# Token tiles between the modulation's pieces, a diagonal product for the norm, and modulation sums as columns, in the opening of a diffusion trunk layer

## The chip, the cores and the metric

The kernel runs on one core of a Trainium2 chip (trn2). Its engines are TensorE (PE; its weight loads are listed apart as PEld), VectorE (DVE), ScalarE (ACT), GpSimd (POOL) and SyncE (SP), which here issues transfers. The metric is the device time of one execution in microseconds (us), of which the median of several runs is taken.

## The reference

One layer of a trunk: the modulation (six vectors of 1024 from `c`, and those of the context from `c_ctx`), a normed and modulated input for 256 context tokens and 1024 latent tokens, one projection, two token mixers, an output projection, and a gated MLP with a depthwise convolution. All is f32.

```python
mod = jax.nn.silu(c) @ ada_w[l] + ada_b[l]
sh1, sc1, g1, sh2, sc2, g2 = [m[:, None, :] for m in jnp.split(mod, 6, axis=-1)]
csh1, csc1, cg1, csh2, csc2, cg2 = jnp.split(jax.nn.silu(c_ctx) @ ada_w[l] + ada_b[l], 6, axis=-1)
hc = modulate(rms_norm(ctx, norm1_g[l]), csh1, csc1)          # x * rsqrt(mean(x*x) + eps) * g, then h * (1 + scale) + shift
out_c, ctx_states = mixer_block(hc, lp, (zero_state, zero_state), not last)
hx = modulate(rms_norm(x, norm1_g[l]), sh1, sc1)
out_x, _ = mixer_block(hx, lp, ctx_states, True)              # starts with h @ lp["w_in"]
x = x + g1 * out_x
...
```

The modulation is (1024) times (1024 x 6144), `ada_w`; only its first third, shift and scale of the first norm, is wanted before the projection. `w_in` is 1024 x 3328.

## The kernel before

The layer is written as stages. This case is about the opening, up to the first projections (L354).

The 1280 tokens lie in ten tiles of 128 tokens (`xt`, 128 x 1024): two of context, eight of latents. `norm_x(i)` takes a tile's mean square on ACT (L267), makes `rstd` on DVE with one square root on ACT (L163 to L175), scales the tile by it on DVE (L269), transposes its eight blocks on TensorE into the banks `ph` (L273), and copies them out, half on ACT, half on DVE (L274). So the tokens come to lie along the free axis, in `raws`, for three segments: context (256 tokens, g = 0) and two of 512 latents (g = 1, 2), each in two halves q of four blocks.

`load_ada(ci, q)` loads one quarter of one of the modulation's four column pieces (`araw`, 128 x 2 x 512, 512 KB; 16 of them). For pieces 0, 1 and 2 TensorE multiplies it: the two columns of `ccs` (silu of `c` and `c_ctx`) are stationary, 512 columns of `araw` move, and the sums come out as two rows (L248). After a piece's last quarter the rows are copied (`arows`, L251) and turned into columns by four small products (`pcol`, L254), and the bias is added (L255) into `modc`. Piece 3 is summed on DVE (`aacc`, L236, L238) and made into columns by products with a vector of ones (L243). With all four, `gs` (L316) is norm gain times (1 + scale).

Then `raws` is modulated: ACT writes the high half of the split operand `hx` (L326, rounded to fp32r), DVE does the same in f32 in place (L327), and the difference is the low half (L328), on POOL for segment 1, on DVE for the others. The projection multiplies, per block of 128 columns of `w_in` and per segment, 8 blocks of the depth by three products: high by high, high by low, low by high (`pj`, L354; 24 products a segment). The first column block is 3072.

Loads are issued by SP in program order; the twelve small parameter loads into `pr` (L278 to L290) by POOL, through the name `PQ`. Tiles `xt` and `araw` share 17 buffers. The order of loads and norms is the string `XO`: a digit is a quarter of that modulation piece, `x` the next token tile, loaded and normed. A scheduler with a timing model of its own orders the instructions on each engine from this program.

Of the kernel before, what the change touches and what calls it, by code (L numbers as in the profile page):

```python
# [8 lines left out]
F32 = mybir.dt.float32  # L9
F32R = mybir.dt.float32r  # L10
AF = mybir.ActivationFunctionType
ALU = mybir.AluOpType
# [25 lines left out]
PADC, PADM = 88, 80  # L38
PN1 = (5,)
NA = 17  # L40
XO = "xx0300301131x123222x"
AE = (0, 1, 0, 1, 0, 0, 1, 0)
B1 = ((4, 5, 1), (2, 3), (6, 7), (0,), (1,))
B2 = ((2, 3), (1, 6))
# [43 lines left out]
def hybrid_kernel(  # L88
# [6 lines left out]
    nc = tc.nc  # L95
    V, A, G, PE, SY = nc.vector, nc.scalar, nc.gpsimd, nc.tensor, nc.sync

    PQ = G
    turns = lambda: tc.manual_schedule(engines={mybir.EngineType.PE})
    E1, E2, E3, ES = G, G, V, V  # L100
    F1, F2, F3, F4 = (V, G), G, G, G
# [25 lines left out]
    ident = cst[:, C_ID:C_ID + 128]  # L127
# [6 lines left out]
    modc = cp.tile([128, 4, 8, 2], F32, name="modc")  # L134
    gs1 = cp.tile([128, 8, 2], F32, name="gs1")
    gs2 = cp.tile([128, 8], F32, name="gs2")
    ccs = cp.tile([128, 8, 2], F32, name="ccs")
# [23 lines left out]
    def rstd_of(pool, ss, n, scale, eps):  # L161
        v = pool.tile([128, n], F32, name="rvar", bufs=2)
        V.tensor_scalar(out=v, in0=ss, scalar1=scale, scalar2=eps, op0=ALU.mult, op1=ALU.add)  # L163
        return newton(pool, v, n)
# [32 lines left out]
    def seg_tile(g, q, b, dt):  # L197
        n = segs3[g][1]
        return (hxp if g else hcp).tile([128, 4, n], dt, name="hx", tag=f"h{g}{q}{b}", bufs=1)
# [6 lines left out]
    with ExitStack() as s2:  # L206
        np_ = s2.enter_context(tc.tile_pool(name="np", bufs=1, side="left", reuse_waits="tile"))
        pp = Banks(pada=(0, 1), padv=(7,), ph=(2, 3, 4, 5), pcol=(6,))
# [5 lines left out]
        xts = []  # L214

        def load_x(i):
            xt = np_.tile([128, D], F32, name="xt", tag="araw", bufs=NA)
            SY.dma_start(xt, ctx[0, i * 128:(i + 1) * 128, :] if i < 2 else x[0, (i - 2) * 128:(i - 1) * 128, :])
            xts.append(xt)
# [4 lines left out]
        def load_ada(ci, q):  # L224
            raw = np_.tile([128, D], F32, name="araw", bufs=NA).rearrange("p (k n) -> p k n", k=2)
            SY.dma_start(raw, ada_w[0, :, ci * 512:(ci + 1) * 512].rearrange("(p k) n -> p k n", k=8)[:, 2 * q:2 * q + 2, :])
            if q == 0:
                adas[ci] = pp.tile([128, 512], F32, name="pada", tag="padv" if ci == 3 else "pada", bufs=2)
            ps = adas[ci]
            bias = prm[:, P_AB + 4 * ci:P_AB + 4 * ci + 4].unsqueeze(2).to_broadcast([128, 4, 2])  # L230
            if ci == 3:
                for kk_ in range(2):
                    for t in range(2):
                        k, z = 2 * q + kk_, acc[t]
                        if k == 0:
                            V.tensor_scalar(out=z, in0=raw[:, kk_, :], scalar1=ccs[:, k, t:t + 1], scalar2=None, op0=ALU.mult)  # L236
                        else:
                            V.scalar_tensor_tensor(out=z, in0=raw[:, kk_, :], scalar=ccs[:, k, t:t + 1], in1=z, op0=ALU.mult, op1=ALU.add)  # L238
                if q == 3:
                    for b in range(4):  # L240
                        for t in range(2):
                            o = ps[:, 2 * b + t:2 * b + t + 1]
                            PE.matmul(o, acc[t][:, 128 * b:128 * b + 128], cst[:, C_ONE:C_ONE + 1], start=True, stop=True)  # L243
                    V.tensor_tensor(out=modc[:, 1, 4:8, :], in0=ps[:, 0:8].rearrange("p (b t) -> p b t", t=2), in1=bias, op=ALU.add)
                return
            for kk_ in range(2):
                k = 2 * q + kk_
                PE.matmul(ps[0:2, :], ccs[:, k, :], raw[:, kk_, :], start=(k == 0), stop=(k == 7))  # L248
            if q == 3:
                rows = np_.tile([2, 512], F32, name="arows", bufs=2)  # L250
                V.tensor_copy(rows, ps[0:2, :])  # L251
                pc = pp.tile([128, 512], F32, name="pcol", tag="pcol", bufs=1)
                for b in range(4):
                    PE.matmul(pc[:, 2 * b:2 * b + 2], rows[:, 128 * b:128 * b + 128], ident[0:2, 0:2], start=True, stop=True)  # L254
                V.tensor_tensor(out=modc[:, ci // 2, 4 * (ci % 2):4 * (ci % 2) + 4, :], in0=pc[:, 0:8].rearrange("p (b t) -> p b t", t=2), in1=bias, op=ALU.add)  # L255

        ss = np_.tile([128, NT], F32, name="ss")
        junk = np_.tile([128, D], mybir.dt.bfloat16, name="junk", bufs=1)
# [5 lines left out]
        def norm_x(i):  # L264
            g = 0 if i < 2 else 1 if i < 6 else 2
            a = 128 * i - segs3[g][0]
            A.activation(junk, xts[i], AF.Square, accum_out=ss[:, i:i + 1])  # L267
            rs = rstd_of(np_, ss[:, i:i + 1], 1, 1.0 / D, eps6)
            V.tensor_scalar(out=xts[i], in0=xts[i], scalar1=rs, scalar2=None, op0=ALU.mult)  # L269
            for q in range(2):  # L270
                ph = pp.tile([128, 4, 128], F32, name="ph", tag="ph", bufs=4)
                for j in range(4):
                    PE.transpose(ph[:, j, :], xts[i][:, 128 * (4 * q + j):128 * (4 * q + j) + 128], ident)  # L273
                (A.copy, V.tensor_copy)[q](raws[g, q][:, :, a:a + 128], ph)  # L274

        pr = np_.tile([128, 3, 128], F32, name="pr")
        V.memset(pr, 0.0)
        PQ.dma_start(pr[0:8, 0, :], norm1_g[0].rearrange("(j p) -> j p", p=128))  # L278
        PQ.dma_start(pr[78:94, 0, :], ada_b[0, 0:2048].rearrange("(j p) -> j p", p=128))
        PQ.dma_start(pr[8:16, 0, :], norm2_g[0].rearrange("(j p) -> j p", p=128))  # L280
        PQ.dma_start(pr[16:20, 0, :], rw_k_k[0].rearrange("(j p) -> j p", p=128))
        PQ.dma_start(pr[20:24, 0, :], rw_k_a[0].rearrange("(j p) -> j p", p=128))
        PQ.dma_start(pr[24:28, 0, :], rw_r_k[0].rearrange("(j a) p -> j (a p)", a=2))
        PQ.dma_start(pr[28:40, 0, :], conv_a_w[0].rearrange("w (j p) -> (w j) p", p=128))
# [13 lines left out]
        V.tensor_copy(prm[:, 161:260], pt[:, 256:355])  # L298
        V.tensor_scalar(out=prm[:, P_LB:P_LB + 16], in0=pt[:, 62:78], scalar1=0.5, scalar2=None, op0=ALU.mult)
        V.tensor_scalar(out=kac, in0=prm[:, P_KA:P_KA + 4], scalar1=-1.0, scalar2=2.0, op0=ALU.mult, op1=ALU.add)  # L300
        n_ = 0
        i_ = [0] * 4
        for o in XO:
            if o == "x":
                load_x(n_)
                norm_x(n_)
                n_ += 1
            else:
                ci = int(o)
                load_ada(ci, i_[ci])  # L310
                i_[ci] += 1
        while n_ < NT:
            load_x(n_)
            norm_x(n_)
            n_ += 1
        V.scalar_tensor_tensor(out=gs1, in0=modc[:, 1], scalar=1.0,  # L316
                               in1=prm[:, P_N1:P_N1 + 8].unsqueeze(2).to_broadcast([128, 8, 2]), op0=ALU.add, op1=ALU.mult)
        for g, (t0, n, w) in enumerate(segs3):
            for q in range(2):
                o = [seg_tile(g, q, i, F32R) for i in range(2)]  # L320
                hxt[g, q, 0], hxt[g, q, 1] = o
                for jj in range(4):
                    j = 4 * q + jj
                    g_, b_ = gs1[:, j, w:w + 1], modc[:, 0, j, w:w + 1]
                    src = raws[g, q][:, jj, :]
                    A.activation(o[0][:, jj, :], src, AF.Identity, scale=g_, bias=b_)  # L326
                    V.tensor_scalar(out=src, in0=src, scalar1=g_, scalar2=b_, op0=ALU.mult, op1=ALU.add)  # L327
                    (G if g == 1 else V).tensor_tensor(out=o[1][:, jj, :], in0=src, in1=o[0][:, jj, :].bitcast(F32), op=ALU.subtract)  # L328


    cols = [3072] + [b + 128 * j for b in (2048, 2560, 1536) for j in range(4)] + [3200]
# [29 lines left out]
    pp = Banks(pj=PJ1, pn=PN1, pv=(4,), pl=PL1)  # L361

    def stg():
        return sg_.tile([128, 512], F32, name="stg", bufs=STG)
# [17 lines left out]
    for d in range(2):  # L382
# [3 lines left out]
        for i, src in enumerate((rw_w_up, rw_a_up)):  # L386
            raw = stg()
# [483 lines left out]
    pp = Banks(pa=B3, ry=(2, 3), pu=(1, 6), **B4)  # L871
# [183 lines left out]
    for r in range(16):  # L1055
# [3 lines left out]
        if r == RC:  # L1059
            fill(999)  # L1060
            sa.close()
            op = so.enter_context(tc.tile_pool(name="op", bufs=1, side="left", reuse_waits="tile"))
# [18 lines left out]
    pp = Banks(ry=(2, 3), pu=(1, 6), **B5)  # L1081
# [48 lines left out]
    for f in (1, 0, *range(2, NF)):  # L1130
# [13 lines left out]
        for tap in range(9):  # L1144
            a_, b_ = divmod(tap, 3)
            src = gp[:, a_:a_ + 16, b_:b_ + 64]
# [8 lines left out]
        for hf, c0, n, t0 in PIECES:  # L1155
            V.tensor_tensor(out=act[:, t0:t0 + n], in0=pv[hf][:, c0:c0 + n],  # L1156
                            in1=acc.rearrange("p r c -> p (r c)")[:, t0:t0 + n], op=ALU.mult)
# [29 lines left out]
    for th in range(2):  # L1187
# [8 lines left out]
        for q in range(4):  # L1196
# [3 lines left out]
            t = 4 * th + q  # L1200
# [10 lines left out]
            rs = rstd_of(ep, s_[:, 0:1], 1, 1.0 / D, eps6)  # L1211
# [39 lines left out]
```

## Time and profile before

| | |
|---|---|
| device time, median of 3 runs | 1708.09 us (1707.33 to 1716.09) |
| device time of the profiled execution | 1706.38 us |
| span of the profiled execution | 1704.6 us |
| TensorE busy | 1557.3 us, 91% of the span, 10639 matmuls |
| DVE, ACT, POOL busy | 67%, 36%, 33% |
| chain that ended last, by engine | PE 68%, DVE 17%, DMA 7% |
| mean granted TensorE clock | 0.94 |

The profile is of one execution, its times count from the span's start. The granted clock is a share of full speed: 1.00 is 2.4 GHz, 0.50 is 1.2 GHz. An engine's idle time costs something only if it lies on the chain of work that ends last.

### The profile page before, as it was taken

The page shows a single profiled execution, that of the slowest core. Times are in us where ns is not written, and L with a number is a line of the kernel's source. Part 1 is how long each engine was busy: PE and PEld are TensorE (multiplying, and loading weights), DVE is VectorE, ACT ScalarE, POOL GpSimd, SP SyncE. Part 2 cuts the span into 40 slices and gives each one's busy share as a digit, 9 for nine tenths or more (in the row PEclk, how much of TensorE's full clock was granted, in tenths as well). Part 3 has the DMA queues.
Part 4 walks back from the last instruction along what each step waited for, and adds up shares of the span by engine and source line. Part 5 has one row for each costly group of instructions (what it writes and reads, how often), then busy time and mean ns, then how long its engine had stood idle before and what let it go on. Part 6 is the DMA issues. An engine that isn't in the chain of part 4 may idle for free.

```text
span 1704.6 us, 27504 instructions
## 1 busy us (share of the span) xinstructions
PE 1557.3 (91%) x10639; PEld 1258.8 (74%) x10639; DVE 1148.5 (67%) x1783; ACT 619.2 (36%) x1158; POOL 562.6 (33%) x489
## 2 busy tenths in 40 slices
PE   7699999989899866899778889999999999999997
PEld 2588768867777656787666668888888888788886
DVE  4954525798899987444677577777777777446645
ACT  2654315544445335444345331211111111324323
POOL 2343312332333303412444322222222222545643
PEclk9699799989799976999889999999999999999999
DMA  9385536557576487988652211111111111533521
GB/s 320 105 292 170 182 95 208 164 152 247 159 231 209 135 248 221 331 249 279 188 164 85 92 50 50 50 50 48 43 46 50 50 50 50 178 106 124 173 93 57
DMA packets 233147, 246.94 MB, mean 145 GB/s; under 512 B 18483, under 2 KB 171656, under 8 KB 233016
## 3 DMA queue, kind: packets, MB, share of 16 engines
q1 hardware_dynamic: 232632, 245.02, 46.1%
q8 instruction: 84, 1.38, 0.3%
q14 instruction: 47, 0.39, 0.1%
q0 software_dynamic: 384, 0.15, 0.0%
HBM read 178.79 MB, written 66.33 MB: 144 GB/s over the span
## 4 chain that ended last, share of the span: by engine, by line
PE 68%; DVE 17%; DMA 7%; ACT 3%; issue 3%; POOL 2%; SPq 1%; DVEq 0%; ACTq 0%; POOLq 0%
PE pf L1104 26%; PE pj L354 13%; PE pf L1184 12%; PE pco L906 2%; DVE ti L672 2%; DVE tmp L670 2%; PE po L906 2%; PE px L601 2%; DMA araw<-in_ada_w_dram 2%; DVE acc L1151 2%; PE ry L760 1%; PE pu L772 1%; PE ps L784 1%; DMA vu<-v_dram 1%; PE ry L752 1%
## 5 line engine op out<-in xcount | busy, mean ns | idle before, releaser
L1104 PE MATMUL pf<-h,fhi 128*128 128x512 f32 x1408 | 385.1, 390 | 6.7 <-DVE act L1156 4.1
L1104 PEld LDWEIGHTS pf<-h,fhi 128*128 128x128 f32 x1408 | 265.0, 188 | 63.1 <-DVE act L1156 4.5
L354 PE MATMUL pj<-hx,whi 128*128 128x512 f32 (+1 forms) x976 | 301.6, 388 | 0.9 <-DVE hx L328 0.9
L1151 DVE SCALAR_TENSOR_TENSOR acc<-gp,prm,acc 128x1024 f32<-128x1024 f32 x176 | 272.7, 1551 | 6.0
L106 POOL TENSOR_TENSOR flo<-fraw,fhi 128x1024 fp32r<-128x1024 f32 x50 | 124.2, 2485 | 306.0 <-ACT fhi L105 305.9
L1104 PE MATMUL pf<-h,flo 128*128 128x512 f32 x704 | 223.7, 390 | 0.0
L354 PEld LDWEIGHTS pj<-hx,whi 128*128 128x128 f32 x976 | 184.0, 196 | 37.2 <-issue 4.2
L354 PE MATMUL pj<-hx,wlo 128*128 128x512 f32 (+1 forms) x488 | 189.0, 388 | 0.0
L1184 PE MATMUL pf<-dhi,ahl 128*128 128x512 f32 x640 | 163.0, 389 | 0.2 <-DVE ahl L1176 0.2
L1176 DVE TENSOR_TENSOR ahl<-act,ahl 128x512 fp32r<-128x512 f32 x44 | 86.2, 1969 | 100.2 <-ACT ahl L1175 100.2
L1104 PEld LDWEIGHTS pf<-h,flo 128*128 128x128 f32 x704 | 132.5, 188 | 27.5 <-POOL flo L106 0.2
L105 ACT CAST fhi<-fraw 128x1024 fp32r<-128x1024 f32 x50 | 52.7, 1054 | 266.7 <-issue 158.6
L1184 PEld LDWEIGHTS pf<-dhi,ahl 128*128 128x128 f32 x640 | 120.0, 188 | 25.5 <-DVE ahl L1176 0.6
L106 POOL TENSOR_TENSOR dlo<-fraw,dhi 128x1024 fp32r<-128x1024 f32 x40 | 98.6, 2469 | 92.2 <-ACT dhi L105 88.2
L106 POOL TENSOR_TENSOR wlo<-wraw,whi 128x1024 fp32r<-128x1024 f32 x26 | 63.6, 2447 | 159.9 <-ACT whi L105 159.8
L354 PEld LDWEIGHTS pj<-hx,wlo 128*128 128x128 f32 x488 | 95.7, 196 | 17.2 <-issue 1.7
L1149 DVE TENSOR_SCALAR acc<-gp,prm 128x1024 f32<-128x1024 f32 x22 | 42.5, 1932 | 97.3 <-ACT gp L1141 97.3
L650 POOL TENSOR_TENSOR car<-car,pcs 128x512 f32<-128x512 f32 (+1 forms) x38 | 39.3, 1046 | 152.4 <-DMA car<-ar_dram 102.1
L1184 PE MATMUL pf<-dlo,ahl 128*128 128x512 f32 x320 | 89.1, 389 | 0.0
L601 PE MATMUL px<-arO,kbO 64*128 64x128 f32 (+1 forms) x640 | 63.9, 310 | 18.1 <-DVE xrO L605 12.7
L105 ACT CAST dhi<-fraw 128x1024 fp32r<-128x1024 f32 x40 | 41.9, 1050 | 105.0 <-PE pf L1184 87.4
L601 PEld LDWEIGHTS px<-arO,kbO 64*128 64x128 f32 x640 | 51.9, 207 | 34.6 <-issue 28.9
(292 smaller groups left out, 2651.2 us busy)
## 6 DMA issues: line engine op xcount, KB each, us to landing
araw<-in_ada_w_dram SPq DMA_DIRECT2D x48, 512.0 KB, 5.5
fraw<-in_ffn_w_up_dram SPq DMA_DIRECT2D x46, 512.0 KB, 3.8
fraw<-in_ffn_w_down_dram SPq DMA_DIRECT2D x44, 512.0 KB, 3.7
wraw<-in_w_in_dram SPq DMA_DIRECT2D x26, 512.0 KB, 4.5
lu<-lu_dram SPq DMA_DIRECT2D x20, 512.0 KB, 5.2
kb_dram<-kbT SPq DMA_DIRECT2D x40, 256.0 KB, 2.6
xa_dram<-xa SPq DMA_DIRECT2D x20, 512.0 KB, 5.6
cxa<-xa_dram SPq DMA_DIRECT2D x40, 256.0 KB, 3.8
```

The lines of the kernel that those rows point to most:

```text
L105: A.copy(hi, src)
L106: G.tensor_tensor(out=lo, in0=src, in1=hi.bitcast(F32), op=ALU.subtract)
L354: PE.matmul(p[:, :n], w[:, k, :], hsl(i, k, t0, n), start=(k == 0 and first), stop=(k == 7 and last))
L601: PE.matmul(px[:, ch, i, 0:w], kbO[r, i, 2 * ch:2 * ch + 2, :].rearrange("p s n -> p (s n)"), rhs, start=True, stop=True)
L650: F3.tensor_tensor(out=self.ar, in0=self.ar, in1=self.pc.to_broadcast(list(self.ar.shape)), op=ALU.mult)
L670: V.tensor_tensor(out=tv, in0=ti[:, j + 1:32, j:j + 1].to_broadcast([128, m, j]), in1=ti[:, j:j + 1, 0:j].to_broadcast([128, m, j]), op=AL ...
L906: m = PE.matmul(po, hl[:, a_, k, :], w[k][b_][:, sl], start=(k == 0 and f), stop=(k == 3 and l))
L1104: PE.matmul(pts[hf], w[:, k, :], h2[hf][i_][:, k, :], start=(k == 0 and f), stop=(k == 7 and l))
L1149: V.tensor_scalar(out=acc, in0=src, scalar1=wcol, scalar2=prm[:, P_FB + f:P_FB + f + 1], op0=ALU.mult, op1=ALU.add)
L1151: V.scalar_tensor_tensor(out=acc, in0=src, scalar=wcol, in1=acc, op0=ALU.mult, op1=ALU.add)
L1176: V.tensor_tensor(out=hl[:, 1, :], in0=asl, in1=hl[:, 0, :].bitcast(F32), op=ALU.subtract)
L1184: PE.matmul(pd[i], hl[:, a_, 128 * q:128 * q + 128], w[w_][:, 512 * nh:512 * nh + 512], start=(f == 0 and s_), stop=(f == NF - 1 and l_))
```

## The change

The token tiles are loaded two ahead of the parameters and then one behind each quarter of pieces 3 and 0; pieces 1 and 2 come last. The norm no longer scales the tile: `rstd` scales an identity matrix (`dg`, 128 x 128), and a product with it transposes and scales at once (L272 of the changed kernel). The modulation's sums for pieces 0, 1 and 2 are made with 128 x 128 blocks of `araw` stationary and the two columns of `ccs` moving, so that they come out as columns (L250); `arows` and `pcol` are gone. The low halves are all on DVE (L334), and for the two latent segments every second block is modulated in place by ACT (L331). The parameter loads are issued by SP.

```diff
-XO = "xx0300301131x123222x"
+XO = "3x0x3x0x3x0x3x0x11112222"
...
-    PQ = G
+    PQ = SY
...
-                PE.matmul(ps[0:2, :], ccs[:, k, :], raw[:, kk_, :], start=(k == 0), stop=(k == 7))
+
+                for b in range(4):
+                    PE.matmul(ps[:, 2 * b:2 * b + 2], raw[:, kk_, 128 * b:128 * b + 128], ccs[:, k, :], start=(k == 0 and b == 0), stop=(k == 7), skip_group_check=True)
             if q == 3:
-                rows = np_.tile([2, 512], F32, name="arows", bufs=2)
-                V.tensor_copy(rows, ps[0:2, :])
-                pc = pp.tile([128, 512], F32, name="pcol", tag="pcol", bufs=1)
-                for b in range(4):
-                    PE.matmul(pc[:, 2 * b:2 * b + 2], rows[:, 128 * b:128 * b + 128], ident[0:2, 0:2], start=True, stop=True)
-                V.tensor_tensor(out=modc[:, ci // 2, 4 * (ci % 2):4 * (ci % 2) + 4, :], in0=pc[:, 0:8].rearrange("p (b t) -> p b t", t=2), in1=bias, op=ALU.add)
+                V.tensor_tensor(out=modc[:, ci // 2, 4 * (ci % 2):4 * (ci % 2) + 4, :], in0=ps[:, 0:8].rearrange("p (b t) -> p b t", t=2), in1=bias, op=ALU.add)
...
-            V.tensor_scalar(out=xts[i], in0=xts[i], scalar1=rs, scalar2=None, op0=ALU.mult)
+
+            dg = np_.tile([128, 128], F32, name="dg", bufs=2)
+            V.tensor_scalar(out=dg, in0=ident, scalar1=rs, scalar2=None, op0=ALU.mult)
...
-                    PE.transpose(ph[:, j, :], xts[i][:, 128 * (4 * q + j):128 * (4 * q + j) + 128], ident)
+                    PE.matmul(ph[:, j, :], xts[i][:, 128 * (4 * q + j):128 * (4 * q + j) + 128], dg, start=True, stop=True)
                 (A.copy, V.tensor_copy)[q](raws[g, q][:, :, a:a + 128], ph)
 
+        for _ in range(2):
+            load_x(len(xts))
...
-        n_ = 0
+        for n_ in range(2):
+            norm_x(n_)
+        n_ = 2
...
-                    V.tensor_scalar(out=src, in0=src, scalar1=g_, scalar2=b_, op0=ALU.mult, op1=ALU.add)
-                    (G if g == 1 else V).tensor_tensor(out=o[1][:, jj, :], in0=src, in1=o[0][:, jj, :].bitcast(F32), op=ALU.subtract)
+                    if g and jj % 2:
+                        A.activation(src, src, AF.Identity, scale=g_, bias=b_)
+                    else:
+                        V.tensor_scalar(out=src, in0=src, scalar1=g_, scalar2=b_, op0=ALU.mult, op1=ALU.add)
+                    V.tensor_tensor(out=o[1][:, jj, :], in0=src, in1=o[0][:, jj, :].bitcast(F32), op=ALU.subtract)
```

In the order lists that follow, a row is a line, an operation, what it writes and reads, the size of what it writes, and how often it stands there in a row.

TensorE at the kernel's start, before the change:

```order
L248 MATMUL pada<-araw,ccs 2x512 x2
L273 MATMUL ph<-cst,xt 128x128 x8
L248 MATMUL pada<-araw,ccs 2x512 x2
L273 MATMUL ph<-cst,xt 128x128 x8
L248 MATMUL pada<-araw,ccs 2x512 x14
L273 MATMUL ph<-cst,xt 128x128 x8
```

The same place in the changed kernel:

```order
L272 MATMUL ph<-dg,xt 128x128 x8
L293 MATMUL ptr<-cst,pr 128x128
L294 MATMUL ptr<-cst,pr 128x128
L272 MATMUL ph<-dg,xt 128x128 x5
L295 MATMUL ptr<-cst,pr 128x128
L272 MATMUL ph<-dg,xt 128x128 x3
L250 MATMUL pada<-ccs,araw 128x2 x16
L272 MATMUL ph<-dg,xt 128x128 x16
L250 MATMUL pada<-ccs,araw 128x2 x5
```

The token tiles have moved ahead of the modulation's sums, and a quarter's two products of 512 columns have become eight of two columns.

TensorE at the end of the opening, before the change, where the modulation's last sums are followed by token tiles and the first projection:

```order
L248 MATMUL pada<-araw,ccs 2x512 x2
L294 MATMUL ptr<-cst,pr 128x128
L254 MATMUL pcol<-cst,arows 128x2 x12
L273 MATMUL ph<-cst,xt 128x128 x16
L354 MATMUL pj<-hx,whi 128x256
L273 MATMUL ph<-cst,xt 128x128 x4
```

The same place in the changed kernel:

```order
L250 MATMUL pada<-ccs,araw 128x2 x4
L272 MATMUL ph<-dg,xt 128x128 x8
L250 MATMUL pada<-ccs,araw 128x2 x4
L272 MATMUL ph<-dg,xt 128x128 x8
L250 MATMUL pada<-ccs,araw 128x2 x64
L360 MATMUL pj<-hx,whi 128x256 x2
L360 MATMUL pj<-hx,wlo 128x256
```

All token tiles now stand ahead of the sums of pieces 1 and 2, 64 products in a row, and the first projection stands behind these.

ACT where the operands are made, in the changed kernel (L329 writes a high half, L331 is the new modulation in place, `xr` and `hx` on the right are the `raws` of a segment):

```order
L105 CAST whi<-wraw 128x1024
L329 ACTIVATE hx<-hx,modc,gs_68 128x256 x4
L329 ACTIVATE hx<-xr_120,modc,gs_68 128x256 x4
L329 ACTIVATE hx<-hx,modc,gs_68 128x512 x8
L329 ACTIVATE hx<-xr_124,modc,gs_68 128x512 x4
L331 ACTIVATE hx<-hx,modc,gs_68 128x512 x4
L331 ACTIVATE xr_124<-xr_124,modc,gs_68 128x512 x2
L329 ACTIVATE hx<-hx,modc,gs_68 128x512 x4
L331 ACTIVATE hx<-hx,modc,gs_68 128x512 x2
```

Nothing of the norm stands between them any more, where before the mean squares and copies of the last token tiles did.

## Rows read from the trace of the kernel before

**Rows 1.** The page's first line.

```profile
span 1704.6 us, 27504 instructions
```

**Rows 2.** The chain of work, 0 to 90 us: start, length, what.

```profile
36.39 8.75 DMA xt<-in_x_dram
...
76.14 13.87 PE pj L354 x72
```

**Rows 3.** Slices of 40 us: busy time (instructions) of each engine, clock, DMA.

```profile
80.00:120.00 40.00, 40.00 (x207) 32.88 (x206) 25.57 (x37) 24.32 (x43) 13.81 (x10) 1.00 0.77 251
...
200.00:240.00 40.00, 40.00 (x174) 27.24 (x174) 15.55 (x28) 7.13 (x13) 8.19 (x5) 0.87 0.34 106
```

**Rows 4.** DVE in order of time, 0 to 90 us: start, length, instruction.

```profile
10.71 0.16 DVE L175 SCALAR_TENSOR_TENSOR rstd<-rstd,rstd 128x1 f32<-128x1 f32 x1
...
45.51 0.17 DVE L316 SCALAR_TENSOR_TENSOR gs<-modc,prm 128x16 f32<-128x16 f32 x1
...
48.16 1.05 DVE L327 TENSOR_SCALAR hx<-hx,gs,modc 128x256 f32<-128x256 f32 x3
...
61.78 1.03 DVE L173 TENSOR_TENSOR rstd<-rstd 128x1 f32<-128x1 f32 x1
...
81.74 1.45 DVE L327 TENSOR_SCALAR xr<-xr,gs,modc 128x512 f32<-128x512 f32 x3
83.11 2.49 DVE L328 TENSOR_TENSOR hx<-xr,hx 128x512 fp32r<-128x512 f32 x4
```

**Rows 5.** POOL in order of time, 0 to 130 us.

```profile
61.30 2.72 POOL L328 TENSOR_TENSOR hx<-hx 128x512 fp32r<-128x512 f32 x2 [0.36 <-DVE hx L327]
```

**Rows 6.** SP's queue in order of time, 0 to 99 us.

```profile
2.60 1.52 SPq L218 DMA_DIRECT2D xt<-in_ctx_dram  x2
...
97.79 0.30 SPq L406 DMA_DIRECT2D bc8f<-in_bcast_dram  x1
```

**Rows 7.** Slices of 2 us of the opening; columns as in rows 3.

```profile
26.00:28.00 2.00, 2.00 (x6) 0.38 (x5) 1.23 (x5) 0.00 (x0) 0.00 (x0) 1.00 1.05 387
...
42.00:44.00 2.00, 1.74 (x10) 1.66 (x9) 1.66 (x11) 1.09 (x2) 0.00 (x0) 0.53 1.01 324
44.00:46.00 2.00, 2.00 (x11) 1.98 (x11) 1.63 (x9) 1.25 (x4) 0.00 (x0) 0.50 1.01 395
```

**Rows 8.** TensorE's groups, 0 to 90 us: shapes, count, busy us, mean ns.

```profile
L273 PE MATMUL ph<-cst,xt 128*128 128x128 f32 x80 | 16.7, 379 | 14.2 <-DVE xt L269 10.6 <-ACT hx L326 3.0 <-ACT hx L274 0.6
...
L254 PE MATMUL pcol<-cst,arows 2*128 2x2 f32 x24 | 4.2, 291 | 1.4 <-DVE prm L299 0.9 <-DVE modc L255 0.5
```

**Rows 9.** TensorE's matmuls in order of time, 0 to 60 us.

```profile
10.23 3.57 PE L248 MATMUL pada<-araw,ccs 128*2 128x512 f32 x4 [10.23 <-ACT rstd L169]
...
15.26 1.88 PE L248 MATMUL pada<-araw,ccs 128*2 128x512 f32 x4
17.07 1.09 PE L273 MATMUL ph<-cst,xt 128*128 128x128 f32 x8
...
33.03 1.95 PE L243 MATMUL pada<-cst,aacc 128*128 128x1 f32 x16
...
40.17 1.02 PE L254 MATMUL pcol<-cst,arows 2*128 2x2 f32 x8 [0.90 <-DVE prm L299]
...
43.00 1.86 PE L254 MATMUL pcol<-cst,arows 2*128 2x2 f32 x8 [0.26 <-DVE modc L255]
```

**Rows 10.** TensorE's matmuls in order of time, 164 to 188 us.

```profile
164.99 0.50 PE L482 MATMUL pada<-cst,acc 128*128 128x1 f32 x4
```

**Rows 11.** Slices of 2 us in a later stage; columns as in rows 3.

```profile
166.00:168.00 2.00, 2.00 (x16) 1.94 (x16) 0.41 (x1) 0.52 (x2) 2.00 (x1) 1.00 0.23 66
168.00:170.00 2.00, 2.00 (x12) 1.97 (x12) 1.30 (x3) 1.80 (x3) 0.71 (x2) 0.60 0.00 1
```

**Rows 12.** ACT in order of time, 40 to 90 us.

```profile
46.28 2.07 ACT L326 ACTIVATE hx<-hx,modc,gs 128x256 fp32r<-128x256 f32 x4
...
76.00 2.94 ACT L326 ACTIVATE hx<-hx,modc,gs 128x512 fp32r<-128x512 f32 x4
```

## The prediction

> **What bounds the kernel now.** I read the page first, for the span, then the chain of work for the opening, then slices of it, then single engines. Sums go against the profiled execution: 1706.38 us device time, 1704.6 us of span [rows 1], 1.7 us below the median of 1708.09. The chain of the opening goes through transfers of the modulation's weights and of token tiles until 45 us, then through norming and transposing the last token tiles, and from 76.14 us on it is `pj` products alone [rows 2]. From there TensorE has no idle time: 40.00 us of 40 in each of the four slices from 80 to 240 us, of which the first and the last are shown [rows 3]. So the change is worth what it does to the moment at which the projections run without gaps. The mark I use: the 72 products that the chain shows from 76.14 end at 90.0 us [rows 2]; with the 24 of the context done earlier, column block 3072 is then complete, and the context part of the next one as well.
>
> Two things hold 76 us up. The modulation is known at 45.5 us (`gs`), but the last token tiles come in behind it, and DVE, which norms them, is slow just then: a 128x1 operation, 0.16 us at 10.71, took 1.03 us at 61.78 [rows 4], while POOL computed the low halves of segment 1 [rows 5].
>
> **The transfers.** In the new order SP issues the context tiles by 4.1 us, then 12 small parameter loads, then the rest. The two context tiles held SP for 1.52 us, a small load of eight rows for 0.30 [rows 6]; 12, two of them of 99 rows, cost 4 to 6 us, so the first modulation piece is issued at about 9 and moves at about 10 us. At 387 GB/s [rows 7] a tile of 0.524 MB takes 1.36 us. Up to the last modulation piece there are 24 such tiles, one weight tile and six of a quarter: 36 us. It lands at 46 to 48 us, about where the modulation is complete now. The parameter loads leave POOL, where they were hidden. The last token tile, 16th in this row, lands at 32 us.
>
> **TensorE in the opening.** Here the change adds. The order lists count f32 products; the trace shows each of them as two matmuls with two weight loads: the first two products of L248 in the list are x4 at 10.23, the 12 of L254 are x24, but the 80 transposes are x80 [rows 8, 9]. A transposed block of the norm becomes a product, 80 to 160 matmuls. Each modulation piece is now 8 products with 128x128 stationary and 2 moving columns, 16 matmuls of nothing but weight loading: 12 pieces, 192 matmuls. The twin of these in the trace is L243 (128x128 stationary, 1 column): 16 in 1.95 us, 0.122 us each, at the upper clock level. The old pieces took 0.47 us for a 512-column matmul (1.88 for four, 15.26), 48 of them; the L254 round trip, 24 matmuls and 4.2 us, goes [rows 8, 9]. For the 128-column matmul of the norm I take 0.122 too; a transpose took 0.136 (17.07) [rows 9]. At the upper level the opening's sum goes from 48 x 0.47 + 80 x 0.136 + 4.2 + 2 = 40 us to (160 + 192 + 16) x 0.122 = 45 us. At the lower level a weight-loading matmul takes 0.233 us (L254 at 43.00: 8 in 1.86, against 0.127 at 40.17) [rows 9], and the new sum is 86 us.
>
> **Which level?** The granted clock decides. Twice in this trace TensorE did weight loads with next to no moving columns, and twice the clock fell. At 40.17 to 44.86 it did L254, with short pauses: 0.53 and 0.50 in the slices 42 to 46 [rows 7, 9]. From 164.99 on it did L482, four matmuls at a time, 128x128 stationary and one column, the new pieces' shape, with some like them between: PE busy is 2.00 of 2.00, PEld 1.94, and yet the slice 168 to 170 stands at 0.60 [rows 10, 11]. What the engine did before each fall was to load weights; with the old 512-column pieces it stood at 1.00, as in the slice 26 to 28 [rows 7]. So I take the lower level for a long run of the new sums.
>
> Now the queue. TensorE can begin at 11 us, when the first tile's norm is ready (L175 at 10.71) [rows 4]. Ahead of the last 64 products stand 160 norm matmuls, 64 of piece 0 and 16 of L243: 240, or 29 us at the upper level. The first 32 run at the lower level, as the first four of the kernel did (3.57 against 1.88 us for the next four [rows 9]): 7.5 us. The next 16 need the seventh transfer, at 20 us, and end at 23. Of the 192 left I take 25 at the lower level and 167 at the upper, since two thirds are norm matmuls, whose nearest rows, the transposes at 17.07, ran there: 5.8 + 20.4 us, to 49 us. All transfers are in by then, so nothing paces the last 64 products but TensorE: 128 matmuls, the first 33 in 4 us at the upper level, as L482's stretch still had it, 95 at 0.233 us, 22 us. The modulation is complete at **75 us**, against 45.5 now. Bounds, both without waits: 56 us all at the upper level (11 + 29 + 15.6), 97 all at the lower (11 + 56 + 30).
>
> **Behind the modulation** the change gains. Nothing of the norm is left to do; ACT does 8 high halves of 256 at 0.52 us and 16 of 512 at 0.73, and now 8 of the 16 in-place blocks of 512 as well: 21.7 us [rows 12]. DVE does 8 x (0.35 + 0.35) for the context, 8 in-place blocks at 0.48 and 16 low halves at 0.62: 19.4 us, with POOL idle, as it was at 81.74 and 83.11 [rows 4]. ACT's last in-place block is ready at 21.7, some six low halves follow on DVE (3.7 us), TensorE is done 1 us later: block 3072 is complete 26 us after the modulation (20 by DVE's sum alone, 28 if all eight low halves of the last segment wait for ACT's end), the context part of the next block (24 of the 72 products, with half the columns of the others: 13.87 x 24/120 us [rows 2]) 2.8 us after that. Now it is 44.5 us from `gs` to that mark; 15.6 us are gained, and in that is what POOL's low halves cost DVE.
>
> **Sum.** 75 + 26 + 2.8 = 104 us for what ends at 90.0 now: 14 us later. Since TensorE then has no gap for 150 us, nothing takes this back. Later stages stand in another order in places, because the scheduler's clock starts elsewhere; the waits there can move by some us either way, and I put 0 +- 5 us, which no row bounds. So 1706.4 + 14 = 1720.4 us, against the median 1722 us.
>
> **Rivals.**
> 1. The loads keep their upper price. Then the last 64 products end 15.6 us after 49, at 64.6, or at 61 to 62 if the queue before was faster too: the mark stands at 90.5 to 93.5, 0 to +4 us, 1708 to 1712 us. For it: the L243 stretch at 33 us ran at 0.122; against it: [rows 10, 11]. The Trainium skill, "TensorE: Matmul & The Clock Gate", section "LDWEIGHTS (loading the stationary operand)", prices a load by its columns alone, 107 ns for 128, and its closing table advises to keep the engine continuously busy for full throughput; by the first the 128 matmuls take 14 us, by the second 15.6 us, and this rival would hold. The L254 loads, 0.127 and then 0.233 us, and L482's stretch disagree here. Chance 0.17.
> 2. TensorE isn't the limit: the sums keep up with the transfers and the modulation is complete at 50 us. Then the mark stands at 79 us, 11 us earlier: 1697 us, faster. This decides if 16 matmuls fit in the 1.36 us of a transfer, 0.085 us each; the nearest row, L243, has 0.122. Chance 0.08.
> 3. The norm stretch doesn't hold the upper level either, since modulation sums stand between its tiles and it waits for DVE. With half of the 167 at the lower level, 9 us more, and all of the last 64 there, 30 us: the modulation at 88 us, the mark 27 us later, 1735 us. For it: the order of the queue, where 5 or 8 weight-loading products stand between most tiles; against it: the backlog, which leaves TensorE no idle time. Chance 0.17.
> 4. The later stages' new order gives back or takes more than 5 us: added to each of the others; alone, 0.05.
>
> **How the numbers follow.** Forecast 0.53, with its own range 1714 to 1730. 0.5% of the median, about what can be told from no change, is 8.5 us. Slower by more: nearly all of the forecast and rival 3, 0.66; within: rival 1, the forecast's low end and half of 4, 0.24; faster: rival 2 and part of 4, 0.10. The range takes rivals 1 and 3 in as far as 1706 and 1737 and leaves 2 out.
>
> **What would show it.** In the new profile: the span's count of matmuls up by about 200; L250 x192, with a mean spacing of 0.2 us or more behind 49 us and a granted clock of 0.50 there; `gs` at 70 to 80 us with the last `araw` landed by 48; no DVE instruction stretched by POOL; 26 us from `gs` to the end of the first 72 `pj` products. Wrong if `gs` stands before 65 us, or if the clock stays at 1.00 while L250 runs alone.

## The result and the profile after

The changed kernel takes 1722.01 us (median of 7 runs, 1717.54 to 1726.03) against 1708.09 us, 1.0082 times as long, with an interval of 1.0058 to 1.0105: slower by 13.9 us. Its profiled execution took 1726.03 us, the slowest of the seven: 4.0 us above the median, and 19.6 us above the profiled execution of before.

The page's first line of the changed kernel, and its TensorE matmuls; the second answers to the count of matmuls that was forecast to rise by about 200 (10639 before):

```profile
span 1724.2 us, 27878 instructions
...
PE 1582.7 (92%) x10839; PEld 1302.3 (76%) x10839; DVE 1146.9 (67%) x1780; ACT 625.0 (36%) x1166; POOL 544.0 (32%) x469
```

The chain of work of the changed kernel, 0 to 110 us (start, length, what), answers to [rows 2]:

```profile
25.46 5.13 PE ph L272 x32
...
44.78 1.89 PE ph L272 x16
46.68 25.01 PE pada L250 x128
71.71 0.18 DVE modc L252
71.91 0.18 DVE gs L319
72.12 12.51 ACT hx L329 x20
84.63 0.71 ACT hx L331
85.36 0.70 DVE hx L334
86.11 14.89 PE pj L360 x68
```

The chain of before went through transfers and the last token tiles. From 25 us on this one is TensorE's alone: the norm is over at 46.7 us, and then the last 128 matmuls of the column sums take 25 us, while the other engines stand nearly still. `gs` ends at 72.1 us in place of 45.7. The mark (the end of the first 96 `pj` matmuls, block 3072 and the context's part of the next) is at 86.11 + 14.89 = 101.0 us in place of 90.0.

Slices of 2 us of the changed kernel; columns as in [rows 3]:

```profile
22.00:24.00 2.00, 2.00 (x10) 2.00 (x11) 1.90 (x13) 0.99 (x2) 0.00 (x0) 0.50 1.04 395
28.00:30.00 2.00, 2.00 (x19) 2.00 (x18) 1.05 (x3) 0.87 (x3) 0.00 (x0) 0.90 1.05 399
38.00:40.00 2.00, 2.00 (x20) 2.00 (x19) 1.01 (x3) 0.59 (x1) 0.00 (x0) 1.00 1.15 267
46.00:48.00 2.00, 2.00 (x22) 2.00 (x20) 0.69 (x1) 0.41 (x1) 0.00 (x0) 1.00 1.03 360
48.00:50.00 2.00, 2.00 (x16) 2.00 (x15) 0.00 (x0) 0.00 (x0) 0.00 (x0) 0.72 1.04 385
50.00:52.00 2.00, 2.00 (x11) 2.00 (x11) 0.00 (x0) 0.00 (x0) 0.00 (x0) 0.50 1.04 285
60.00:62.00 2.00, 2.00 (x11) 2.00 (x11) 0.00 (x0) 0.00 (x0) 0.00 (x0) 0.50 1.15 364
68.00:70.00 2.00, 2.00 (x11) 2.00 (x11) 0.00 (x0) 0.00 (x0) 0.00 (x0) 0.50 0.00 0
80.00:82.00 2.00, 0.78 (x3) 0.29 (x2) 1.96 (x4) 2.00 (x4) 0.00 (x0) 1.00 0.00 0
82.00:84.00 2.00, 0.00 (x0) 0.00 (x0) 1.20 (x3) 2.00 (x4) 0.00 (x0) 0.75 0.00 0
```

Read the second figure behind the window, PE's busy time, beside its count. TensorE is busy for 2.00 of 2.00 us both at 46 us and at 68 us, but it does 22 matmuls in the one and 11 in the other: the busy share says nothing of the speed, the granted clock beside it does, 1.00 and 0.50. VectorE, ScalarE and POOL stand at 0.00 in the slices shown from 50 us to 70. The first transfers of the opening end at 52 us (0.11 in the next slice), so they don't pace it. From 80.8 to 86.1 us TensorE waits for a low half on DVE (L334 at 85.36), which waits for ACT's first block in place (L331 at 84.63).

TensorE's matmuls of the changed kernel in order of time (start, length of the group, line, shapes, count), answering to [rows 9]:

```profile
10.86 3.78 PE L272 MATMUL ph<-dg,xt 128*128 128x128 f32 x16 [10.86 <-DVE dg L268]
...
16.70 1.92 PE L250 MATMUL pada<-ccs,araw 128*128 128x2 f32 x16
21.89 3.57 PE L250 MATMUL pada<-ccs,araw 128*128 128x2 f32 x16 [3.27 <-DMA araw<-in_ada_w_dram]
25.32 5.27 PE L272 MATMUL ph<-dg,xt 128*128 128x128 f32 x32
...
44.65 2.03 PE L272 MATMUL ph<-dg,xt 128*128 128x128 f32 x16
46.51 25.16 PE L250 MATMUL pada<-ccs,araw 128*128 128x2 f32 x128
```

The same 16 matmuls of the column sums take 1.92 us at 16.70 and 3.57 us at 21.89. Within the last group the starts of single matmuls are 0.112 us apart until 48.9 us, but for the first two (0.03), and 0.213 us apart behind.

### The profile page after: what moved, and what is told of

Read it like the earlier page. It is cut to its first block, busy times and chain, and to the rows that moved or that the text cites. A ratio compares the mean times of both kernels' runs of the same rounds, so it can differ in the third digit from the quotient of the medians.

```text
span 1724.2 us, 27878 instructions
## 1 busy us (share of the span) xinstructions
PE 1582.7 (92%) x10839; PEld 1302.3 (76%) x10839; DVE 1146.9 (67%) x1780; ACT 625.0 (36%) x1166; POOL 544.0 (32%) x469
## 4 chain that ended last, share of the span: by engine, by line
PE 68%; DVE 21%; DMA 4%; ACT 3%; issue 2%; POOL 1%; SPq 1%; DVEq 0%; ACTq 0%; POOLq 0%
PE pf L1110 26%; PE pf L1190 12%; PE pj L360 11%; DVE ti L678 3%; DVE tmp L676 3%; PE po L912 2%; PE pco L912 2%; PE pada L250 2%; DVE acc L1157 2%; PE ry L766 2%; PE pu L778 1%; PE ps L790 1%; PE ph L272 1%; PE px L607 1%; DVE xrO L611 1%
## 5 line engine op out<-in xcount | busy, mean ns | idle before, releaser
L360 PE MATMUL pj<-hx,whi 128*128 128x512 f32 (+1 forms) x976 | 307.0, 393 | 6.8 <-DVE hx L334 5.7
L360 PEld LDWEIGHTS pj<-hx,whi 128*128 128x128 f32 x976 | 187.8, 200 | 46.3 <-DVE hx L334 6.7
L607 PE MATMUL px<-arO,kbO 64*128 64x128 f32 (+1 forms) x640 | 62.4, 304 | 13.9 <-DVE xrO L611 9.8
```

What stands on the lines that cost most here:

```text
L360: PE.matmul(p[:, :n], w[:, k, :], hsl(i, k, t0, n), start=(k == 0 and first), stop=(k == 7 and last))
L607: PE.matmul(px[:, ch, i, 0:w], kbO[r, i, 2 * ch:2 * ch + 2, :].rearrange("p s n -> p (s n)"), rhs, start=True, stop=True)
```

## The experiments

The theory (A): the modulation's sums, as 128-column weight loads with two moving columns, make TensorE the limit of the opening, and in a long run of them its clock falls to the lower level. The rivals, whose letters change from run to run: that the loss lies in the token tiles and the order of later stages (B in the first four runs), that the loads cost what they do at any clock (B in wide_columns), that the transfers set the end, or that the diagonal product or the low halves carry the loss. Each ratio is against runs of the kernel before taken beside it (their medians lie between 1708.09 and 1709.63 us, so medians of different rows compare to 1.5 us only); "mark" is as above, from the profiled execution (90.0 us before).

| kernel | `gs` ends, us | mark, us | median, us | ratio (interval) |
|---|---|---|---|---|
| changed kernel | 72.1 | 101.0 | 1722.01 | 1.0082 (1.0058 to 1.0105) |
| rows | 63.7 | 92.5 | 1706.71 | 0.9981 (0.9971 to 0.9991) |
| columns | 60.1 | 95.0 | 1708.77 | 0.9991 (0.998 to 1.0002) |
| rows_transposes | 59.6 | 88.4 | 1707.93 | 0.9995 (0.998 to 1.0011) |
| mixed | 69.1 | 98.1 | 1715.99 | 1.0052 (1.0028 to 1.0075) |
| transposes | 75.2 | 104.0 | 1719.47 | 1.0059 (1.0039 to 1.0079) |
| pool_params | 65.8 | 94.7 | 1713.87 | 1.003 (1.0014 to 1.0046) |
| pool_lows | 71.6 | 104.4 | 1726.22 | 1.0103 (1.0087 to 1.0118) |
| lows_only | 46.9 | 94.0 | 1714.41 | 1.0038 (1.0023 to 1.0052) |
| wide_columns | 61.2 | 90.3 | 1708.34 | 0.9999 (0.9988 to 1.001) |
| wide_columns_pool | 55.4 | 84.6 | 1699.49 | 0.9949 (0.9933 to 0.9965) |
| rows_pool | 59.9 | 89.3 | 1709.3 | 0.9999 (0.9983 to 1.0016) |
| rows_transposes_pool | 56.6 | 86.7 | 1703.66 | 0.9967 (0.9955 to 0.9979) |

**rows**: the changed kernel with the row sums of before (and their round trip through `pcol`).

```diff
-  for b in range(4):
-      PE.matmul(ps[:, 2 * b:2 * b + 2], raw[:, kk_, 128 * b:128 * b + 128], ccs[:, k, :], ...)
+  PE.matmul(ps[0:2, :], ccs[:, k, :], raw[:, kk_, :], start=(k == 0), stop=(k == 7))
...
```

> The changed kernel with the modulation's sums made as rows again (512 moving columns, then the four small products and the copy), all else as changed. Theory A (the column sums, all weight loads at the lower clock level, hold up the modulation): the token tiles still end at about 46 us, then 26 matmuls of 512 columns in 0.43 us each, 11 us, and 4 us for the round trip: modulation complete at 61 us in place of 71.9, time 1711 us, granted clock 1.00 in that stretch. Rival B (the loss lies in the token tiles ahead of the modulation and in the order of later stages, not in the sums): 1722 us, within 3.

Theory A, with a time 4 us under its 1711 and a `gs` 2.7 us behind its 61. Of the time the whole loss went: undoing the column sums alone gives 1706.71 us. The new order, the diagonal products and the low halves stay in it, so none of these need carry the 13.9 us. At the mark 8.5 of the 11.0 us went; the 2.5 that stay there don't show in the time. The last sums in its chain, 26 matmuls of 512 columns, and `gs`:

```profile
49.79 11.25 PE pada L248 x26
...
63.56 0.19 DVE gs L322
```

**columns**: the kernel before with the column sums alone (the same edit the other way).

> The kernel before with the column sums alone. Theory A: 192 weight-loading matmuls, most at 0.195 us, end at 54 to 56 us where the modulation is complete at 45.5 before, and the token tiles' transposes stand behind them: 8 to 11 us longer, 1716 to 1719 us. Rival B: 1708 us, within 3.

A's number missed: the mark moved by only 5.0 us and the time not at all. With before's order the token tiles are normed behind the modulation anyway, until 74 us, and cover most of what the sums cost: behind `gs` its chain goes through DVE, until 84.8 us. In these two orders the sums are dear where they stand last. What the later stages gave back here is not explained.

**rows_transposes**: the changed kernel with row sums, the scaling on VectorE and transposes, so that the order and the low halves remain.

```diff
-  dg = np_.tile([128, 128], F32, name="dg", bufs=2)
-  V.tensor_scalar(out=dg, in0=ident, scalar1=rs, scalar2=None, op0=ALU.mult)
+  V.tensor_scalar(out=xts[i], in0=xts[i], scalar1=rs, scalar2=None, op0=ALU.mult)
...
-  PE.matmul(ph[:, j, :], xts[i][...], dg, start=True, stop=True)
+  PE.transpose(ph[:, j, :], xts[i][...], ident)
```

> The changed kernel with row sums, and with the tile scaled on DVE and transposed as before; the order of loads, the low halves and the parameter loads as changed. Theory A: TensorE no longer limits; the modulation is complete 4 us after its last piece lands at about 50 us, at 55 us, and 29 us later stands the mark that was at 90 before and at 101 as changed: 84 us. Time 1703 to 1706 us, less than the kernel before. Rival B: 1722 us, within 3.

A's numbers missed here: it had `gs` at 55, the mark at 84 and 1703 to 1706 us. B's 1722 us is far off. With row sums the diagonal product moves the mark by 92.5 - 88.4 = 4.1 us and the time not measurably.

**mixed**: the changed kernel with another order: two pieces, then token tiles between the rest, a token tile between the last pieces too.

```diff
-XO = "3x0x3x0x3x0x3x0x11112222"
+XO = "30303030x1x1x1x1x2x2x2x2"
```

> The changed kernel with one thing different, the order of loads: pieces 3 and 0 first, then each token tile ahead of a quarter of pieces 1 and 2, so that norm products and column sums alternate on TensorE to the end. The same instructions. Theory A, the clock holds in the mixture: 256 matmuls at 0.122 us from about 23 us on, modulation complete at 56 to 58 us, 1708 us. Theory A, the clock falls in the mixture: 256 at 0.21, complete at 78 us, 1728 us. Rival B gives no number here: 1715 to 1722 us.

In between: +8.1 us at the mark, and a time that B's range has too. The clock settles what the time leaves open: it fell in the run of 68 matmuls of column sums and 16 of L243 that now stands ahead of the tiles (0.50 from 22.3 to 35.9 us), and at the end, where the sums alternate with diagonal products, it stood at 1.00, and 16 matmuls of the sums take 1.68 to 1.73 us, in place of 3.4 at 0.50:

```profile
62.00:64.00 2.00, 2.00 (x21) 2.00 (x20) 0.53 (x1) 0.59 (x1) 0.00 (x0) 1.00 0.00 0
```

What it lost again: TensorE stands idle from 51 to 56 us, for ACT's copy of a tile (L273), which stands behind the cast of a weight tile that lands at 54.4 us.

**transposes**: the changed kernel with scaling and transposes for the diagonal product; the column sums stay (the diff of rows_transposes alone).

> The changed kernel with the norm by a multiply on VectorE and transposes again; the column sums stay. Theory A (the opening is bound by TensorE's weight loads, two for each diagonal product, one for each transpose): 104 loads and moving passes of about 0.12 us fewer before the modulation's last sums, so gs ends at 62 to 68 us in place of 72.1, block 3072 at 92 to 98 us in place of 101, time about 1716 us (1712 to 1719). Rival B (the diagonal product costs nothing, the column sums at the lower level of the clock cost all): gs at 71 to 72, 1721 to 1723 us. Rival C (each of the two parts fits alone, and only both together overload TensorE): the whole loss goes, 1707 to 1710 us.

None of the three: `gs` is later, at 75.2 us, though 80 matmuls are gone; the time, 1719.47 us, lies between A's and B's. TensorE's matmuls of this kernel in order of time, and two of its slices:

```profile
20.39 1.95 PE L270 MATMUL ph<-cst,xt 128*128 128x128 f32 x8
22.17 3.57 PE L250 MATMUL pada<-ccs,araw 128*128 128x2 f32 x16
...
45.76 3.65 PE L270 MATMUL ph<-cst,xt 128*128 128x128 f32 x16
49.21 25.60 PE L250 MATMUL pada<-ccs,araw 128*128 128x2 f32 x120
```

```profile
40.00:42.00 2.00, 2.00 (x11) 2.00 (x10) 0.82 (x2) 1.53 (x2) 0.61 (x1) 1.00 1.04 266
...
60.00:62.00 2.00, 2.00 (x11) 2.00 (x11) 0.17 (x1) 0.00 (x0) 0.00 (x0) 1.00 1.09 342
```

Here the clock column must not be believed. It says 1.00, but a matmul takes 0.213 to 0.22 us from start to tail, 11 in 2 us, as at 0.50 in the changed kernel; not until the projections, at 82.0 us, does a 256-column matmul fall from 0.41 to 0.28 us. The column shows 1.00 from the start of a profile to the first recorded change, which in this trace is a rise at 82.0 us; the changed kernel's first 16 matmuls took 3.78 us under a 1.00 too. So I read the level from the durations: with transposes and column sums alone TensorE never rose. The diagonal product doubles the matmuls of the norm, but in this kernel it also is what brought the clock up at 28 to 30 us, and the two cancel, but for 3 us. The Trainium skill, "TensorE: Matmul & The Clock Gate", section "Part 4: PE-mode transpose", says that the upper level doesn't engage for transposes. This opening agrees with it, and so does that of columns (82 matmuls of column sums in 17.49 us, 0.213 each, no rise before 65 us), but neither tests it alone: column sums stand between the transposes, and these let the clock fall by themselves in the changed kernel's tail.

**pool_params**: the changed kernel with the twelve parameter loads on POOL's queue, as before.

```diff
-    PQ = SY
+    PQ = G
```

> The changed kernel with the parameter rows loaded by POOL's queue again, so that the first modulation piece is issued by SP some 3 us earlier. Theory A (TensorE is the limit of the opening from 30 us on, the transfers have slack): gs ends within 1 us of 72, time 1720 to 1723 us. Rival (the transfers set the opening's end): gs 3 us earlier, 1718 to 1719 us.

Both expectations missed; the move of these loads to SP cost more than I had allowed, 6.3 us at the mark and 8.1 us of the median (9.7 when each is taken against the runs of before beside it). The chain of this kernel, 30 to 100 us, and a slice to set beside the changed kernel's:

```profile
40.42 24.96 PE pada L250 x128
65.38 0.02 issue
65.41 0.18 DVE modc L252
```

```profile
22.00:24.00 2.00, 2.00 (x19) 2.00 (x20) 1.96 (x7) 0.95 (x3) 0.00 (x0) 1.00 1.06 407
```

The tail is as long as before, but begins at 40.4 in place of 46.7 us. The first modulation piece is issued at 4.14 us in place of 10.13, so TensorE has no 3.27 us of idle time at 18 to 22 us; it stays at the upper level through the stretch where the changed kernel had 0.50 (22 to 28 us), and does the norm 6 us sooner. TensorE was the limit, and yet a transfer that came late at the start set it back.

**pool_lows**: the changed kernel with the old block of low halves (all scalings on VectorE, segment 1's subtractions on POOL).

> The changed kernel with the old block of low halves (all scalings on VectorE, subtractions of the middle segment on POOL). Theory A (the stage from gs to block 3072 takes 29 us either way, since ScalarE's high halves of 12.5 us come first in it): 1720 to 1724 us. Rival B (POOL's subtractions slow VectorE and end late): the stage 4 us longer, about 1726 us. Rival C (the second scalings on ScalarE made TensorE wait 5.7 us for the low halves): 3 to 5 us shorter, 1717 to 1719 us.

Rival B: the stage from `gs` to the mark takes 104.4 - 71.6 = 32.8 us in place of 28.9. POOL and VectorE in order of time in this kernel, one row of each, and a row of VectorE in the changed kernel:

```profile
79.71 10.09 POOL L331 TENSOR_TENSOR hx<-hx 128x512 fp32r<-128x512 f32 x7 [0.37 <-DVE hx L330]
```

```profile
82.86 4.37 DVE L330 TENSOR_SCALAR hx<-hx,gs,modc 128x512 f32<-128x512 f32 x3
```

```profile
89.60 0.55 DVE L333 TENSOR_SCALAR hx<-hx,gs,modc 128x512 f32<-128x512 f32 x1 [1.43 <-ACT hx L329]
```

While POOL subtracts (79.7 to 89.8 us), a scaling on VectorE takes 1.5 us; the changed kernel's, without POOL, takes 0.55. This part of the change is worth some 4 us where it was put.

**lows_only**: the kernel before with the new low-half block alone.

> The kernel before with the new block of low halves alone. Theory A (the stage is covered by TensorE's norm stretch and projections, so the block's engine does not matter): block 3072 ends at 90 +- 1.5 us, time within 2 us of the kernel before. Rival B (ScalarE, which copies and squares the token tiles there, is late with the scalings too): block 3072 3 to 6 us later, 1711 to 1714 us. Rival C (POOL's share was the late one): 2 to 4 us earlier, 1704 to 1706 us.

Rival B: the mark is 4.0 us later and the time 0.38% longer. In this order ScalarE still copies and squares token tiles, the last copy at 76.5 us. The chain then goes through ScalarE's high halves of the last segment and its scaling, and TensorE waits for them until 84.4 us:

```profile
76.51 0.59 ACT hx L274
77.13 5.75 ACT hx L326 x8
82.88 0.71 ACT hx L328
83.62 0.70 DVE hx L331
84.37 25.72 PE pj L357 x126
```

So the same edit loses 4 us in the old order and gains 4 in the new.

**wide_columns**: the changed kernel with the two silu columns repeated 64 times, so that each column product moves 128 columns; the loads are the same, and two result columns of 128 are read.

```diff
+        ccw = np_.tile([128, 8, 128], F32, name="ccw")
+        V.tensor_copy(ccw.rearrange("p k (r t) -> p k r t", t=2), ccs.unsqueeze(2).to_broadcast([128, 8, 64, 2]))
...
-      PE.matmul(ps[:, 2 * b:2 * b + 2], raw[:, kk_, 128 * b:128 * b + 128], ccs[:, k, :], ...)
+      PE.matmul(ps[:, 128 * b:128 * b + 128], raw[:, kk_, 128 * b:128 * b + 128], ccw[:, k, :], ...)
...
```

> The changed kernel with 128 columns moved in each column product in place of 2 (the two silu columns repeated 64 times; same sums, same number of weight loads, only 2 of the 128 result columns are read). Theory A (what the column sums cost is the fall of TensorE's clock: 0.195 us a pair in the tail at 0.50, 0.105 to 0.118 us at 1.00, and it falls because 2 columns a load keep it too little occupied): the tail's 128 pairs take 128 x 0.118 = 15.1 us in place of 25.2, the granted clock stays at 1.00 through them, gs ends at 59 to 63 us, block 3072 at 88 to 92 us, time 1709 to 1712 us. Rival B (the loads themselves cost 0.2 us in a long run, and moving columns only add to it): the tail takes 25 to 40 us, gs at 72 or later, 1722 to 1735 us.

Theory A, with a time 0.7 us under its range. The chain of this kernel, and slices of its tail:

```profile
43.40 3.57 PE ph L274 x32
46.97 13.86 PE pada L252 x124
```

```profile
48.00:50.00 2.00, 2.00 (x20) 2.00 (x20) 0.00 (x0) 0.00 (x0) 0.00 (x0) 1.00 1.05 388
50.00:52.00 2.00, 2.00 (x20) 2.00 (x20) 0.00 (x0) 0.00 (x0) 0.00 (x0) 1.00 1.11 326
...
58.00:60.00 2.00, 2.00 (x21) 2.00 (x20) 0.00 (x0) 0.00 (x0) 0.78 (x2) 1.00 0.45 125
```

The tail begins at 47.0 us, as in the changed kernel (46.7), has the same weight loads, moves 64 times as many columns, and takes 13.9 us for the 124 that stand last, where 128 took 25.0. The clock stays at 1.00, where it fell 2.3 us into the tail with two columns. The mark is 10.7 us earlier, the median 13.7.

**wide_columns_pool, rows_pool, rows_transposes_pool**: the three better ones with the parameter loads on POOL's queue.

> The same with the parameter rows on POOL's queue. Theory A: the tail starts at 40 us as with the parameter rows on POOL alone and ends at 55 to 57 us, or when the last transfer of 50 us allows; block 3072 at 84 to 87 us, 1702 to 1707 us. Rival B: gs at 65 to 80 us, 1714 to 1725 us.

> The changed kernel with row sums, and the parameter rows on POOL's queue, so that the first modulation piece is issued at 4 us in place of 10. Theory A (TensorE starts its norm stretch 6 us earlier and stays ahead; the sums still end last): gs at 58 to 60 us in place of 63.7, block 3072 at 87 to 89 us, 1701 to 1704 us. Rival (the order of later stages decides as much): as the kernel with row sums, 1706 to 1707 us.

> The changed kernel with row sums and transposes, and the parameter rows on POOL's queue. Theory A: gs at 54 to 57 us in place of 59.6, block 3072 at 83 to 86 us, 1702 to 1705 us. Rival (without the diagonal products TensorE's clock does not rise early, and the stretch runs at 0.50): gs at 60 to 66 us, 1708 to 1713 us.

The first beats both kernels, by 8.8 us the one before: all parts of the change but the parameter loads, with 128 columns moved. Its chain:

```profile
42.06 12.97 PE pada L252 x116
...
55.25 0.18 DVE gs L321
55.46 12.56 ACT hx L331 x20
```

A's time for it, 1702 to 1707 us, was too high; its mark is inside. rows_pool gained 3.2 us at the mark and nothing in the time: a miss for A, and its 1709.3 us is above the rival's 1706 to 1707 as well; rows_transposes_pool's time is inside A's range and its mark 0.7 us outside.

## Why the prediction came out

The forecast was 1722 us and the median is 1722.01; its steps were off by a few us each, some of which cancelled.

- **Transfers.** The first modulation piece was issued at 10.1 us, against about 9. The wait for the seventh transfer was in the sum (20 us; it ended at 21.9), but not what it costs to have these loads in front: pool_params puts it at 6.3 us of the 11.0 at the mark.
- **The queue ahead of the tail** ended at 46.7 us, against 49. Of the first 32 matmuls, all taken at the lower level, 16 ran there (3.78 us) and 16 at the upper. Of the 192 from 21.9 us on, 30 ran at the lower level, against 25 taken, and the others at 0.112 to 0.118 us, against 0.122.
- **The tail** took 25.0 us, against 26. The clock fell after 2.3 us, not 4, with 22 matmuls started, and 106 x 0.213 = 22.6 us followed; 0.233 was taken. That the fall in the long run of sums makes the cost is shown by wide_columns: the same loads with the clock kept up take 13.9 us. Rival 1 would have been right at the upper price throughout. The Trainium skill, "TensorE: Matmul & The Clock Gate", section "LDWEIGHTS (loading the stationary operand)", which spoke for it, has 107 ns for 128 columns. The rows show nearly that from matmul to matmul at 1.00 (112 ns) and twice as much at 0.50 (213 ns).
- **The modulation** was complete at 72, against 75; rival 2's 50 is far off. Rival 3 (norm stretch at the lower level too) did not come in the changed kernel, but transposes shows how near it is: without the diagonal products the whole opening runs at the lower level.
- **From `gs` to the mark** 28.9 us, against 28.8, but in part by another way. In the step TensorE ends 1 us behind the last low halves. In the trace it waits until 86.1 us for a low half of the first latent segment, behind ACT's first block in place, and then does 68 matmuls without a gap in 14.9 us; the last low half, done at 96.4 us, doesn't hold it.
- **Mark** +11.0, against +14; **later stages** +2.9 by the medians, against 0 +- 5. By the two profiled executions, of which the marks are, it is 19.6 - 11.0 = 8.6 us, outside the 5: in these the first product of the MLP (`pf`) starts at 945.1 us in place of 927.5. Over the thirteen kernels of the table the shift of the median (against the runs of before beside it) and that of the mark differ by between -5.4 (columns) and +2.9 us (the changed kernel), with either sign. What makes these few us is not settled: no run changed the later stages alone. The forecast's hit on the median is thus partly luck; on the mark it was 3 us too high.

Not told apart in the forecast: the parameter loads' move alone makes 8.1 us of the 13.9, and 6.3 of the 11.0 at the mark (pool_params); the column sums make all of the time, and 8.5 at the mark (rows). The two don't add, since beside row sums taking the loads off SP again gave 3.2 us at the mark and nothing in the time (rows_pool). The order and the new low halves together are no loss (rows_transposes: mark 88.4 us, ratio 0.9995).

## What to carry to other kernels

Before turning a wide matmul round to save a round trip, count what it becomes: a product that loads 128 columns to move two is all weight load, and a run of them can halve the clock of the engine that stands last. Moving more columns with the same loads, useless ones too, can then be cheaper than moving few. A small load moved to the head of another queue is paid by whoever waits for the first big transfer behind it.

## What the runs showed of the hardware

- An f32 matmul with 128 loaded columns takes 0.112 us, from start to start, with two moving columns and with 128 when the granted clock is 1.00 (changed kernel, wide_columns): 126 more moving columns are free there. At 0.50 it takes 0.213, with two.
- PE and PEld busy at 2.00 of 2.00 us did not keep the clock up: 22 us at 0.50 in the changed kernel's tail. With 128 moving columns at the same busy share it stayed at 1.00 (wide_columns).
- Transposes with column sums between them never brought the level up before the projections (columns, transposes); with 512-column row sums between the same transposes it rose (rows_transposes, 16 transposes in 1.81 us).
- The clock column shows 1.00 ahead of the first recorded change, whatever the level is; durations of one shape have to be read beside it.
